# Batched experts on one core: two experts' weight matrices in one transfer, layers in pairs of experts

## The chip, the core and the metric

The kernel runs on one core of a Trainium2 chip. The time is that of one execution on the device, in microseconds (us); the lower the better. Several executions give a median. Beside them one execution was recorded by the hardware profiler, and every row below is from that one.

Five engines work side by side and meet at semaphores: TensorE (PE, matmuls; its weight loads are PEld), VectorE (DVE), ScalarE (ACT), GpSimd (POOL) and SyncE (SP). POOL and SP also issue DMA transfers, which 16 DMA engines carry out. An issuing engine takes its instructions in order: a transfer that must wait for a buffer holds up all that stands behind it in the same engine's list.

## What is computed

Eight experts, each a two-layer network with a ReLU between, on 256 rows each:

```
x  : 8 x 256 x 512     w1 : 8 x 512 x 2048     w2 : 8 x 2048 x 512     (all f32)
h   = relu(x[e] @ w1[e])
out[e] = h @ w2[e]                                                     (f32)
```

One weight matrix of one expert is 4.19 MB in f32. There are sixteen of them, 67.1 MB; x is another 4.19 MB and the output 4.19 MB. On the chip the weights, x and h are held in bf16, so a matrix takes 2.1 MB (the profile's "2048 KB"), 16 KB of each of 128 partitions. A transfer issued by POOL converts f32 to bf16 on the way; one issued by SP doesn't.

## The kernel before

**Loads.** `load_w1(e)` (line 69) brings w1 of one expert with one transfer, `load_w2(e)` (line 75) w2 of one expert; w2 of experts 6 and 7 comes in two pieces each. All go out on POOL's queue and are served one after the other. w1 and w2 have a pool of three buffers each (`WB = 3`), so six matrices of 2.1 MB can be on the chip or on their way. The fourth w1 can only be issued when the first layer of expert 0 has read its buffer, and so on.

**x.** x comes in groups (`GROUPS`): expert 0 alone, expert 1 alone, 2 and 3, 4 to 7. Experts 0 and 1 come through SP in f32 with one transfer each (line 145) and are cast to bf16 on ACT (lines 155 and 156); the others come through POOL (line 65). `transpose_x(g)` turns a group with PE transposes and copies the result out of PSUM on DVE and ACT.

**Layers.** `first_layer(e)` makes 64 matmuls of 256 columns (line 110) into four PSUM tiles, each of which ACT or DVE writes out with the ReLU as part of `ht[e]`, bf16. `second_layer(e)` makes 32 matmuls of 512 columns (line 130) into two PSUM tiles, which DVE and ACT copy (lines 137 and 138) into `o_sb`, f32. `ht` has three buffers.

**Stores.** The last 16 partitions of expert 0 leave through SP (line 169). Experts 1 to 4 (line 141) and the other 112 partitions of expert 0 (line 190) leave through POOL's queue, issued after the last weights. Experts 5 to 7 leave in one transfer through SP at the very end (line 193).

**Order.** The order is written out by hand, and each engine takes its own instructions in the order of the text. On PE, leaving out transposes: first 0, second 0, first 1, second 1, first 2, second 2, first 3, second 3, first 4, second 4, first 5, first 6, first 7, second 5, second 6, second 7. On POOL's queue: w1 0, w2 0, x of 2 and 3, w1 1, w2 1, x of 4 to 7, w1 2, w2 2, w1 3, w2 3, w1 4, w2 4, w1 5, w1 6, w1 7, w2 5, w2 6 (two pieces), w2 7 (two pieces), then the two stores.

Of the kernel before, what the change touches and what calls it, by code (L numbers as in the profile page):

```python
# [9 lines left out]
@with_exitstack  # L10
def kernel(
    ctx: ExitStack,
    tc: tile.TileContext,
    x: bass.AP,
    w1: bass.AP,
    w2: bass.AP,
    out: bass.AP,
):
    nc = tc.nc
    P = 128  # L20
    bf = mybir.dt.bfloat16
    f32 = mybir.dt.float32
    relu = mybir.ActivationFunctionType.Relu

    E, C, H = x.shape
    F = w1.shape[2]
    MT = C // P
    KT1 = H // P
    KT2 = F // P
    FB = 4  # L30
    WB = 3


    GROUPS = ((0, 1), (1, 1), (2, 2), (4, 4))


    w1_r = w1.rearrange("e (p kt) n -> e p kt n", p=P)
    w2_r = w2.rearrange("e (p kt) n -> e p kt n", p=P)
    out_r = out.rearrange("e (p mt) n -> p e mt n", p=P)

    const = ctx.enter_context(tc.tile_pool(name="const", bufs=1))
    wpool = ctx.enter_context(tc.tile_pool(name="weights", bufs=WB))
    hpool = ctx.enter_context(tc.tile_pool(name="hidden", bufs=3))
    ps_h = ctx.enter_context(tc.tile_pool(name="ps_h", bufs=2, space=bass.MemoryType.PSUM))
    ps_o = ctx.enter_context(tc.tile_pool(name="ps_o", bufs=4, space=bass.MemoryType.PSUM))


    ctx.enter_context(tc.manual_schedule())

    w1_sb, w2_sb, ht = {}, {}, {}  # L50
    group_of = {e: g for g, (e0, n) in enumerate(GROUPS) for e in range(e0, e0 + n)}
    x_f = const.tile([P, 2, MT, H], f32, name="x_f")
    x_b = [const.tile([P, n * MT, H], bf, name=f"x_b{g}") for g, (_, n) in enumerate(GROUPS)]
    xt = [const.tile([P, KT1, MT, n * P], bf, name=f"xt{g}") for g, (_, n) in enumerate(GROUPS)]
    o_sb = const.tile([P, E, MT, H], f32, name="out_sb")
    identity = const.tile([P, P], bf, name="identity")

    def x_rows(g):
        e0, n = GROUPS[g]
        return x[e0:e0 + n].rearrange("e c k -> (e c) k").rearrange(  # L60
            "(p j) k -> p j k", p=P
        )

    def load_x(g):
        nc.gpsimd.dma_start(x_b[g][:], x_rows(g))  # L65

    def load_w1(e):
        w1_sb[e] = wpool.tile([P, KT1, F], bf, tag="w1", name="w1_sb")
        nc.gpsimd.dma_start(w1_sb[e][:], w1_r[e])  # L69

    def load_w2(e):
        w2_sb[e] = wpool.tile([P, KT2, H], bf, tag="w2", name="w2_sb")
        cuts = {E - 2: (0, 8, 16), E - 1: (0, 9, 16)}.get(e, (0, KT2))
        for lo, hi in zip(cuts, cuts[1:]):
            nc.gpsimd.dma_start(w2_sb[e][:, lo:hi, :], w2_r[e, :, lo:hi, :])  # L75

    def transpose_x(g, blocks=None):


        n = GROUPS[g][1]  # L80
        J = n * MT
        KB = 8 // J
        for b in blocks if blocks is not None else range(KT1 // KB):
            pt = ps_o.tile([P, KB, J, P], bf, tag="ps_o", name="pt_tr")
            for i in range(KB):
                for j in range(J):
                    nc.tensor.transpose(  # L87
                        pt[:, i, j, :], x_b[g][:, j, b * KB + i::KT1], identity[:]
                    )
            for i in range(KB) if n > 1 else (slice(0, KB),):  # L90
                if n > 1:
                    src = pt[:, i].rearrange("p (l m) q -> p l m q", m=MT)
                    dst = xt[g][:, b * KB + i].rearrange("p m (q l) -> p l m q", l=n)
                    flip = b * KB + i
                else:
                    src, dst, flip = pt[:, i], xt[g][:], g
                if flip % 2:
                    nc.scalar.copy(dst, src)  # L98
                else:
                    nc.vector.tensor_copy(dst, src)  # L100

    def first_layer(e, between=()):
        g = group_of[e]
        i0 = (e - GROUPS[g][0]) * P
        ht[e] = hpool.tile([P, KT2, C], bf, tag="ht", name="ht_sb")
        for q in range(KT2 // FB):
            ph = ps_h.tile([P, FB, C], f32, tag="ps_h", name="pt_h")
            for i in range(FB):
                for kt in range(KT1):
                    nc.tensor.matmul(  # L110
                        ph[:, i, :],
                        w1_sb[e][:, kt, FB * q + i::KT2],
                        xt[g][:, kt, :, i0:i0 + P],
                        start=(kt == 0),
                        stop=(kt == KT1 - 1),
                    )
            if q % 2:
                nc.vector.tensor_relu(ht[e][:, FB * q:FB * (q + 1), :], ph[:])  # L118
            else:
                nc.scalar.activation(ht[e][:, FB * q:FB * (q + 1), :], ph[:], relu)  # L120
            if between:
                between.pop(0)()

    def second_layer(e):
        po = [
            ps_o.tile([P, H], f32, tag="ps_o", name=f"pt_o{mt}") for mt in range(MT)
        ]
        for kt in range(KT2):
            for mt in range(MT):
                nc.tensor.matmul(  # L130
                    po[mt][:],
                    ht[e][:, kt, mt * P:(mt + 1) * P],
                    w2_sb[e][:, kt, :],
                    start=(kt == 0),
                    stop=(kt == KT2 - 1),
                )
        nc.vector.tensor_copy(o_sb[:, e, 0, :], po[0][:])  # L137
        nc.scalar.copy(o_sb[:, e, 1, :], po[1][:])  # L138

    def store(e0, e1):  # L140
        nc.gpsimd.dma_start(out_r[:, e0:e1], o_sb[:, e0:e1])  # L141


    for e in (0, 1):
        nc.sync.dma_start(x_f[:, e], x_rows(e))
    load_w1(0)
    make_identity(nc, identity)
    load_w2(0)
    load_x(2)
    load_w1(1)  # L150
    load_w2(1)
    load_x(3)
    load_w1(2)
    load_w2(2)
    nc.scalar.copy(x_b[0][:], x_f[:, 0])  # L155
    nc.scalar.copy(x_b[1][:], x_f[:, 1])  # L156
    transpose_x(0)

    first_layer(0)
    load_w1(3)  # L160
    transpose_x(1)
    second_layer(0)
    load_w2(3)
    first_layer(1)
    load_w1(4)
    transpose_x(2)
    second_layer(1)
    for p in range(112, P, 4):
        nc.sync.dma_start(out_r[p:p + 4, 0], o_sb[p:p + 4, 0])
    load_w2(4)  # L170
    first_layer(2, [lambda kt=kt: transpose_x(3, [kt]) for kt in range(KT1)])
    load_w1(5)
    second_layer(2)
    first_layer(3)
    load_w1(6)
    second_layer(3)
    first_layer(4)
    load_w1(7)
    load_w2(5)
    load_w2(6)  # L180
    second_layer(4)
    load_w2(7)


    for e in (5, 6, 7):
        first_layer(e)


    store(1, 5)
    nc.gpsimd.dma_start(out_r[:112, 0], o_sb[:112, 0])  # L190
    for e in (5, 6, 7):
        second_layer(e)
    nc.sync.dma_start(out_r[:, 5:8], o_sb[:, 5:8])


# [28 lines left out]
```

## Time and profile before

| | |
|---|---|
| median of the runs | 183.04 us |
| the three runs | 183.12, 181.7, 183.04 us |
| span of the profiled execution | 180.0 us |
| PE busy | 127.5 us (71%) in 825 instructions |
| PEld busy | 90.1 us (50%) |
| DVE / ACT busy | 31.8 / 31.6 us (18% each) |
| POOL busy | 12.7 us (7%) |
| chain that ended last, by engine | DMA 45%, PE 40%, unknown queue 8% |

The span runs from the first recorded instruction to the last event of the execution; the time of a run also holds what lies before and after it. PE's busy time is a modelled one, and its idle time matters only where the end of the program waits for it. The rows of the profile that bear on the change are shown in the prediction. In a timeline row stand the start, the duration, engine and line, operation, tile written <- tiles read, the count, and in brackets the idle time before it with what ended it. In a row of windows stand the stretch, its length, each engine's busy time with its instruction count, the granted TensorE clock (1.00 is full), the mean busy share of the DMA engines and the GB/s that they moved, counted on the side of the chip's own memory (bf16 for weights).

### The profile page before, as it was taken

How to read it: one execution, taken by the hardware profiler on the slowest of the kernel's cores; microseconds unless marked ns; L12 is line 12 of the kernel's file. 1: busy time of each engine (PE TensorE's matmuls, PEld its weight loads, DVE VectorE, ACT ScalarE, POOL GpSimd, SP SyncE). 2: the span in 40 equal slices, each digit the busy share in tenths (PEclk: the TensorE clock that was granted, in tenths of full speed). 3: DMA queues.
4: the chain of work that ended last, by engine and by line, in shares of the span. 5: the costliest groups of instructions: out<-in, count | busy, mean ns of one | idle time of the engine just before them, and what ended most of it. 6: DMA issues, size and time to landing. Idle time of an engine off the chain costs nothing.

```text
span 180.0 us, 1823 instructions
## 1 busy us (share of the span) xinstructions
PE 127.5 (71%) x825; PEld 90.1 (50%) x832; DVE 31.8 (18%) x29; ACT 31.6 (18%) x32; POOL 12.7 (7%) x28
## 2 busy tenths in 40 slices
PE   0206999059993199987869497949895876997930
PEld 0105964048840189637723395428795873442410
DVE  0100220101411018610401022010423050101010
ACT  3300240102231026612200022012222220101010
POOL 7300010100101000100100004021010000000000
PEclk9999999957999659999999789996999999999995
DMA  5998998999999999999999999999999999999996
GB/s 210 256 226 182 233 229 178 233 211 215 200 244 204 222 218 208 218 215 229 204 222 218 218 211 211 229 208 222 215 222 208 215 215 204 224 213 209 334 411 248
DMA packets 4262, 40.47 MB, mean 225 GB/s; under 512 B 416, under 2 KB 416, under 8 KB 1952
## 3 DMA queue, kind: packets, MB, share of 16 engines
q0 software_dynamic: 3536, 37.68, 95.7%
q1 hardware_dynamic: 720, 2.69, 3.9%
q8 instruction: 6, 0.10, 0.2%
HBM read 71.30 MB, written 4.19 MB: 419 GB/s over the span
## 4 chain that ended last, share of the span: by engine, by line
DMA 45%; PE 40%; another core or an unknown queue 8%; POOL 1%; issue 1%; ACT 0%; POOLq 0%
DMA w_sb<-in_w_dram 45%; PE pt_o L130 19%; PE pt_h L110 19%; PE pt_tr L87 2%; POOL w_sb L69 0%; ACT out_sb L138 0%; POOL x_b L65 0%; POOL w_sb L75 0%; POOL identity masks.py:199 0%; POOL identity masks.py:197 0%; POOLq masks.py:199 0%; POOLq L208 0%
## 5 line engine op out<-in xcount | busy, mean ns | idle before, releaser
L110 PE MATMUL pt_h<-xt,w_sb 128*128 128x256 bf16 x512 | 67.6, 299 | 31.9 <-DMA w_sb<-in_w_dram 31.9
L110 PEld LDWEIGHTS <-w_sb 128*128 128x128 bf16 x512 | 60.9, 148 | 39.1 <-DMA w_sb<-in_w_dram 35.0
L130 PE MATMUL pt_o<-w_sb,ht_sb 128*128 128x512 bf16 x249 | 56.2, 379 | 7.9 <-DMA w_sb<-in_w_dram 7.4
L130 PEld LDWEIGHTS <-ht_sb 128*128 128x128 bf16 x256 | 24.9, 98 | 37.4 <-issue 7.2
L118 DVE TENSOR_SCALAR ht_sb<-pt_h 128x1024 bf16<-128x1024 f32 x16 | 19.7, 1229 | 69.3 <-PE pt_h L110 69.3
L120 ACT ACTIVATE ht_sb<-pt_h 128x1024 bf16<-128x1024 f32 x16 | 16.5, 1031 | 72.6 <-PE pt_h L110 72.6
L138 ACT COPY out_sb<-pt_o 128x512 f32<-128x512 f32 x8 | 4.7, 586 | 58.9 <-PE pt_o L130 58.9
L137 DVE COPY out_sb<-pt_o 128x512 f32<-128x512 f32 x8 | 5.5, 692 | 53.6 <-PE pt_o L130 53.6
L69 POOL DMA_DIRECT2D w_sb<-in_w_dram x8 | 4.4, 556 | 87.4 <-PE pt_h L110 86.6
L100 DVE COPY xt<-pt_tr 128x1024 bf16<-128x1024 bf16 (+1 forms) x5 | 7.1, 1449 | 18.2 <-PE pt_tr L87 18.2
L87 PE MATMUL pt_tr<-identity,x_b 128*128 128x128 bf16 x64 | 5.6, 242 | 5.3 <-ACT x_b L155 5.3
L98 ACT COPY xt<-pt_tr 128x1024 bf16<-128x1024 bf16 (+1 forms) x5 | 7.4, 1494 | 6.9 <-PE pt_tr L87 4.3
L87 PEld LDWEIGHTS <-x_b 128*128 128x128 bf16 x64 | 4.9, 121 | 5.4 <-ACT x_b L155 5.3
L75 POOL DMA_DIRECT2D w_sb<-in_w_dram x10 | 5.4, 547 | 20.3 <-PE pt_o L130 20.3
L155 ACT CAST x_b<-x_f 128x1024 bf16<-128x1024 f32 x1 | 1.0, 1045 | 2.1 <-DMA x_f<-in_x_dram 2.1
L155 ACT ACT_TABLE_LOAD x1 | 1.3, 1283 | 0.7 <-PEq L208 0.7
L190 POOL DMA_DIRECT2D out_dram<-out_sb x1 | 0.5, 545 | 8.6 <-DMA w_sb<-in_w_dram 8.6
L65 POOL DMA_DIRECT2D x_b<-in_x_dram x2 | 1.1, 550 | 0.0
L156 ACT CAST x_b<-x_f 128x1024 bf16<-128x1024 f32 x1 | 1.0, 1047 | 0.1
L141 POOL DMA_DIRECT2D out_dram<-out_sb x1 | 0.8, 768 | 1.8 <-DMA w_sb<-in_w_dram 1.8
masks.py:199 POOL TENSOR_SCALAR_AFFINE_SELECT identity<-identity 128x128 bf16<-128x128 bf16 x1 | 0.3, 288 | 0.1
masks.py:197 POOL MEMSET identity<- 128x128 bf16 x1 | 0.2, 225 | 0.0
(4 smaller groups left out, 0.4 us busy)
## 6 DMA issues: line engine op xcount, KB each, us to landing
w_sb<-in_w_dram POOLq DMA_DIRECT2D x14, 2048.0 KB, 45.4
w_sb<-in_w_dram POOLq DMA_DIRECT2D x2, 1024.0 KB, 45.4
out_dram<-out_sb POOLq DMA_DIRECT2D x1, 2048.0 KB, 53.0
out_dram<-out_sb SPq DMA_DIRECT2D x1, 1536.0 KB, 6.0
w_sb<-in_w_dram POOLq DMA_DIRECT2D x1, 1152.0 KB, 46.6
x_f<-in_x_dram SPq DMA_DIRECT2D x2, 512.0 KB, 3.7
x_b<-in_x_dram POOLq DMA_DIRECT2D x1, 1024.0 KB, 47.9
w_sb<-in_w_dram POOLq DMA_DIRECT2D x1, 896.0 KB, 50.3
```

Of the source, the lines that this page charges most:

```text
L69: nc.gpsimd.dma_start(w1_sb[e][:], w1_r[e])
L75: nc.gpsimd.dma_start(w2_sb[e][:, lo:hi, :], w2_r[e, :, lo:hi, :])
L87: nc.tensor.transpose(pt[:, i, j, :], x_b[g][:, j, b * KB + i::KT1], identity[:])
L98: nc.scalar.copy(dst, src)
L100: nc.vector.tensor_copy(dst, src)
L110: nc.tensor.matmul(ph[:, i, :], w1_sb[e][:, kt, FB * q + i::KT2], xt[g][:, kt, :, i0:i0 + P], start=(kt == 0), stop=(kt == KT1 - 1),)
L118: nc.vector.tensor_relu(ht[e][:, FB * q:FB * (q + 1), :], ph[:])
L120: nc.scalar.activation(ht[e][:, FB * q:FB * (q + 1), :], ph[:], relu)
L130: nc.tensor.matmul(po[mt][:], ht[e][:, kt, mt * P:(mt + 1) * P], w2_sb[e][:, kt, :], start=(kt == 0), stop=(kt == KT2 - 1),)
L137: nc.vector.tensor_copy(o_sb[:, e, 0, :], po[0][:])
L138: nc.scalar.copy(o_sb[:, e, 1, :], po[1][:])
L155: nc.scalar.copy(x_b[0][:], x_f[:, 0])
```

## The change

The three buffers for w1 and the three for w2 become three buffers of double size with one common tag; each holds the same matrix of two neighbouring experts. `load_w1(e)` and `load_w2(e)` bring both experts with one transfer; only w2 of 6 and 7 still comes as three pieces (6 whole, 7 in two) into one double buffer. The groups of x are 0 and 1, 2 and 3, 4 to 7; x of experts 0 and 1 comes with one transfer on SP and is cast with one instruction. `ht` has four buffers in place of three. On PE the layers run in pairs: first 0, first 1, second 0, second 1, first 2, first 3, second 2, second 3, first 4, first 5, first 6, first 7, second 4, second 5, second 6, second 7. On POOL's queue: w1 of 0 and 1, w2 of 0 and 1, x of 2 and 3, w1 of 2 and 3, w2 of 2 and 3, x of 4 to 7, w1 of 4 and 5, w1 of 6 and 7, w2 of 4 and 5, w2 of 6, w2 of 7 (two pieces), then the two stores as before. The three double buffers are taken in turn, so the fourth transfer (w2 of 2 and 3) waits for the first layer of expert 1, the fifth for the second layer of expert 1, the sixth for the first layer of expert 3, the seventh for the second layer of expert 3, and w2 of 6 and 7 for the first layer of expert 5.

```diff
-    GROUPS = ((0, 1), (1, 1), (2, 2), (4, 4))
+    PAIR = 2
+    GROUPS = ((0, 2), (2, 2), (4, 4))
...
-    hpool = ctx.enter_context(tc.tile_pool(name="hidden", bufs=3))
+    hpool = ctx.enter_context(tc.tile_pool(name="hidden", bufs=4))
...
-    x_f = const.tile([P, 2, MT, H], f32, name="x_f")
+    x_f = const.tile([P, 2 * MT, H], f32, name="x_f")
...
-    def load_w1(e):
-        w1_sb[e] = wpool.tile([P, KT1, F], bf, tag="w1", name="w1_sb")
-        nc.gpsimd.dma_start(w1_sb[e][:], w1_r[e])
+    def pair_tile():
+        return wpool.tile([P, PAIR, KT1 * F], bf, tag="w", name="w_sb")
+
+    def load_w1(e):
+        w = pair_tile()
+        nc.gpsimd.dma_start(
+            w[:], w1_r[e:e + PAIR].rearrange("e p kt n -> p e (kt n)")
+        )
+        for i in range(PAIR):
+            w1_sb[e + i] = w[:, i].rearrange("p (kt n) -> p kt n", n=F)
...
-    def load_w2(e):
-        w2_sb[e] = wpool.tile([P, KT2, H], bf, tag="w2", name="w2_sb")
-        cuts = {E - 2: (0, 8, 16), E - 1: (0, 9, 16)}.get(e, (0, KT2))
-        for lo, hi in zip(cuts, cuts[1:]):
-            nc.gpsimd.dma_start(w2_sb[e][:, lo:hi, :], w2_r[e, :, lo:hi, :])
+    def load_w2(e, cuts=None):
+        w = pair_tile()
+        for i in range(PAIR):
+            w2_sb[e + i] = w[:, i].rearrange("p (kt n) -> p kt n", n=H)
+        if cuts is None:
+            nc.gpsimd.dma_start(
+                w[:], w2_r[e:e + PAIR].rearrange("e p kt n -> p e (kt n)")
+            )
+            return
+        for i, lo, hi in cuts:
+            nc.gpsimd.dma_start(w2_sb[e + i][:, lo:hi, :], w2_r[e + i, :, lo:hi, :])
...
+    nc.sync.dma_start(x_f[:], x_rows(0))
+    load_w1(0)
+    make_identity(nc, identity)
+    load_w2(0)
+    load_x(1)
+    load_w1(2)
+    nc.scalar.copy(x_b[0][:], x_f[:])
+    transpose_x(0)
+    first_layer(0)
+    first_layer(1)
+    load_w2(2)
+    load_x(2)
+    second_layer(0)
+    second_layer(1)
+    load_w1(4)
+    for p in range(112, P, 4):
+        nc.sync.dma_start(out_r[p:p + 4, 0], o_sb[p:p + 4, 0])
+    transpose_x(1)
+    first_layer(2)
+    first_layer(3)
+    load_w1(6)
+    second_layer(2)
+    second_layer(3)
+    load_w2(4)
+    transpose_x(2)
+    first_layer(4)
+    first_layer(5)
+    load_w2(6, ((0, 0, 16), (1, 0, 9), (1, 9, 16)))
+    first_layer(6)
+    first_layer(7)
+    second_layer(4)
+    second_layer(5)
+    store(1, 5)
+    nc.gpsimd.dma_start(out_r[:112, 0], o_sb[:112, 0])
+    second_layer(6)
+    second_layer(7)
+    nc.sync.dma_start(out_r[:, 5:8], o_sb[:, 5:8])
```

The second-layer and first-layer functions are the same in both kernels; `transpose_x` loses the branch for groups of one expert.

More of the change, by code (lines that the diff above doesn't have):

```diff
@@ L141, in store @@
         nc.gpsimd.dma_start(out_r[:, e0:e1], o_sb[:, e0:e1])
-    for e in (0, 1):
-        nc.sync.dma_start(x_f[:, e], x_rows(e))
+    nc.sync.dma_start(x_f[:], x_rows(0))
     load_w1(0)
@@ L148 @@
     load_w2(0)
[L149 to L152, printed above, removed]
+    load_x(1)
     load_w1(2)
-    load_w2(2)
-    nc.scalar.copy(x_b[0][:], x_f[:, 0])
-    nc.scalar.copy(x_b[1][:], x_f[:, 1])
+    nc.scalar.copy(x_b[0][:], x_f[:])
     transpose_x(0)
     first_layer(0)
-    load_w1(3)
-    transpose_x(1)
+    first_layer(1)
+    load_w2(2)
+    load_x(2)
     second_layer(0)
-    load_w2(3)
-    first_layer(1)
+    second_layer(1)
     load_w1(4)
-    transpose_x(2)
-    second_layer(1)
     for p in range(112, P, 4):
         nc.sync.dma_start(out_r[p:p + 4, 0], o_sb[p:p + 4, 0])
[L170 to L173, printed above, removed]
+    transpose_x(1)
+    first_layer(2)
     first_layer(3)
     load_w1(6)
+    second_layer(2)
     second_layer(3)
+    load_w2(4)
+    transpose_x(2)
     first_layer(4)
-    load_w1(7)
-    load_w2(5)
-    load_w2(6)
+    first_layer(5)
+    load_w2(6, ((0, 0, 16), (1, 0, 9), (1, 9, 16)))
+    first_layer(6)
+    first_layer(7)
     second_layer(4)
-    load_w2(7)
-    for e in (5, 6, 7):
-        first_layer(e)
+    second_layer(5)
     store(1, 5)
     nc.gpsimd.dma_start(out_r[:112, 0], o_sb[:112, 0])
-    for e in (5, 6, 7):
-        second_layer(e)
+    second_layer(6)
+    second_layer(7)
     nc.sync.dma_start(out_r[:, 5:8], o_sb[:, 5:8])
```

12 lines of the change are left out of this document (4 added, 8 removed).

## The prediction

> **What bounds the kernel now.** I read the busy shares by slice first, then TensorE's timeline, then POOL's, then the last microseconds.
>
> ```profile
> DMA  5998998999999999999999999999999999999996
> GB/s 210 256 226 182 233 229 178 233 211 215 200 244 204 222 218 208 218 215 229 204 222 218 218 211 211 229 208 222 215 222 208 215 215 204 224 213 209 334 411 248
> q0 software_dynamic: 3536, 37.68, 95.7%
> HBM read 71.30 MB, written 4.19 MB: 419 GB/s over the span
> ```
>
> The DMA engines are full in nearly every slice, and 95.7% of their time is POOL's queue, the weights. The 210 to 220 GB/s are counted in bf16; on the HBM side it is twice that. So the kernel is bound by the stream of weights, and TensorE waits for it:
>
> ```profile
> 15.08 9.16 PE L110 MATMUL pt_h<-xt,w_sb 128*128 128x256 bf16 x64 [8.78 <-DMA w_sb<-in_w_dram]
> ...
> 37.95 9.65 PE L110 MATMUL pt_h<-xt,w_sb 128*128 128x256 bf16 x64 [6.08 <-DMA w_sb<-in_w_dram]
> ...
> 62.36 3.63 PE L110 MATMUL pt_h<-xt,w_sb 128*128 128x256 bf16 x16 [6.96 <-DMA w_sb<-in_w_dram]
> ...
> 81.95 7.22 PE L110 MATMUL pt_h<-xt,w_sb 128*128 128x256 bf16 x64 [1.48 <-DMA w_sb<-in_w_dram]
> 91.65 7.07 PE L130 MATMUL pt_o<-w_sb,ht_sb 128*128 128x512 bf16 x31 [2.48 <-DMA w_sb<-in_w_dram]
> 101.32 8.71 PE L110 MATMUL pt_h<-xt,w_sb 128*128 128x256 bf16 x64 [2.60 <-DMA w_sb<-in_w_dram]
> 111.00 7.07 PE L130 MATMUL pt_o<-w_sb,ht_sb 128*128 128x512 bf16 x31 [0.97 <-DMA w_sb<-in_w_dram]
> 120.68 8.87 PE L110 MATMUL pt_h<-xt,w_sb 128*128 128x256 bf16 x64 [2.61 <-DMA w_sb<-in_w_dram]
> 130.40 7.21 PE L110 MATMUL pt_h<-xt,w_sb 128*128 128x256 bf16 x64 [0.85 <-DMA w_sb<-in_w_dram]
> 140.11 7.21 PE L110 MATMUL pt_h<-xt,w_sb 128*128 128x256 bf16 x64 [2.50 <-DMA w_sb<-in_w_dram]
> 149.79 13.97 PE L130 MATMUL pt_o<-w_sb,ht_sb 128*128 128x512 bf16 x62 [2.47 <-DMA w_sb<-in_w_dram]
> 165.00 4.06 PE L130 MATMUL pt_o<-w_sb,ht_sb 128*128 128x512 bf16 x18 [1.24 <-DMA w_sb<-in_w_dram]
> 169.26 3.18 PE L130 MATMUL pt_o<-w_sb,ht_sb 128*128 128x512 bf16 x14 [0.20 <-DMA w_sb<-in_w_dram]
> ```
>
> Each row's start is the landing of a matrix, so these rows are the clock of the stream. From 111.00 (w2 of 4) to 149.79 (w2 of 5) four matrices land, one per 9.70 us: 4.19 MB in 9.7 us is 432 GB/s, without a gap. A first layer takes 7.2 us at full clock and a second layer 7.0 (13.97 for two; a few matmul records are missing), so TensorE needs 14.2 us per expert while the stream needs 19.4: TensorE is ahead. What counts is how much of TensorE's work is left when the stream ends. Before, all is done behind the last piece (169.26) but 14 matmuls, 3.18 us.
>
> **The stream after the change.** The same bytes go through the same queue. Is it ever dry? A transfer is issued when its buffer comes free:
>
> ```profile
> 2.45 0.55 POOL L75 DMA_DIRECT2D w_sb<-in_w_dram  x1
> ...
> 24.53 0.54 POOL L69 DMA_DIRECT2D w_sb<-in_w_dram  x1 [18.35 <-PE pt_h L110]
> ...
> 121.27 0.77 POOL L141 DMA_DIRECT2D out_dram<-out_sb  x1 [1.85 <-DMA w_sb<-in_w_dram]
> w_sb<-in_w_dram POOLq DMA_DIRECT2D x14, 2048.0 KB, 45.4
> ```
>
> A weight transfer lands 45.4 us (median) after its issue, so nearly five matrices are always queued. I date the pairs by counting bytes. In units of one matrix (9.7 us; x of experts 4 to 7 is half a unit, 4.85): w1 of 0 and 1 is one unit behind 15.08, so 24.8; w2 of 0 and 1 44.1. At 62.36 five matrices and all of x had landed; w1 of 2 and 3 is six without x of 4 to 7, so 62.36 + 9.7 - 4.85 = 67.2. w2 of 2 and 3 is eight, without that x: 91.65 - 4.85 = 86.8. w1 of 4 and 5 is ten matrices and all x, as 111.00 was; w1 of 6 and 7 is twelve, as 130.40 was; w2 of 4 and 5 is fourteen, the same set of bytes but for order as at 149.79; w2 of 7 ends at 169.26 again.
>
> Now the buffers. First layers 0 and 1 end at 24.8 + 9.2 + 7.2 = 41.2 and let w2 of 2 and 3 out; what is queued lasts to 67.2. Second layers 0 and 1 end at 44.1 + 14.0 = 58.1 (w1 of 4 and 5 is needed at 91.6, when x of 4 to 7 is through); first layers 2 and 3 at 67.2 + 9.65 + 7.2 = 84.1 (needed 111.0); second layers 2 and 3 at 100.8 (needed 130.4); first layers 4 and 5 at 111.0 + 9.65 + 7.2 = 127.9 (needed 149.8). The smallest reserve is 21.9 us, the last one. So the start of TensorE at 24.8 in place of 15.08 costs nothing: the queue covers it. If that cover were gone, the missing microseconds would be added one to one.
>
> **Edits of no or little price.** x of 0 and 1 as one transfer and one cast:
>
> ```profile
> 4.16 1.04 ACT L155 CAST x_b<-x_f 128x1024 bf16<-128x1024 f32 x1 [2.13 <-DMA x_f<-in_x_dram]
> ```
>
> This was over at 5.2 and is now needed at 24.8, so a later landing and a longer cast cost nothing. Fewer issues: POOL is not on the path. A pair has 256 runs of 16 KB where one matrix had 128; the store of line 141, with 512 shorter ones, took 0.77 us to issue beside 0.55, so a pair costs at most 0.2 us more, once, at the start. Sum: 0 to 0.2, I take 0. The stores of line 141 and 190 now wait on POOL for second layer 4 (about 159 in place of 121.27), with no load behind them and before 169.26, so they keep their place in the queue. On SP the small stores of line 169 wait for second layer 0 of the new order (about 51); only the last store stands behind them. That the stream loses or wins up to 1.1 us at its beginning (15.08 + two and a quarter units is 36.9, the row says 37.95) stays as an uncertainty of 1.1 either way.
>
> Fewer transfers in the stream: behind 149.79 two matrices came as four pieces and took 19.47 us to 169.26, beside 19.40 for two whole ones; an extra piece costs 0.04 us. Seven fewer transfers before w2 of 4 and 5 (14 become 7): 0.3 us won. [...]
>
> **The tail, where the price is.** At 149.8 before, TensorE had three second layers to do (5, 6, 7), paced by the stream. After the change second layer 4 stands behind first layer 7 too, and w2 of 4 comes only with w2 of 5: four remain, and nothing of them can start earlier. Four at 13.97 per two are 27.9 us. w2 of 6 (159.5) and of 7 (169.26) have landed by the time they are wanted (163.8 and 170.8 at the earliest), so TensorE is now the bound of the end.
>
> And it starts cold. Stretches of the first layers of 1 and 4 and of the three last second layers:
>
> ```profile
> 37.95:48.30 10.35, 10.35 (x80) 9.18 (x81) 1.88 (x2) 2.05 (x2) 0.40 (x1) 0.75 0.99 212
> 101.32:111.00 9.68, 8.71 (x64) 7.88 (x65) 2.15 (x2) 2.05 (x2) 0.67 (x2) 0.84 1.02 217
> 149.79:165.00 15.21, 13.87 (x63) 6.17 (x64) 1.38 (x2) 1.17 (x2) 0.00 (x0) 1.00 1.02 214
> ```
>
> Behind an idle gap of 6.08 us the granted clock was 0.75 over the stretch and the 64 matmuls took 9.65 in place of 7.21 (2.44 lost); behind 2.60, 8.71 (1.5 lost); behind 2.47 and 2.50 nothing. In the tail, first layer 6 starts at 130.4 after a gap of 2.5 (7.2 to 8.9 us), first layer 7 ends at 144.8 to 146.5, and the gap to 149.8 is 3.3 to 5.0 us: between the rows that lost 1.5 and 2.44. I take 2.0, bounds 0 and 2.5.
>
> The end of TensorE: 149.8 + 27.9 + 2.0 = 179.7. Behind it:
>
> ```profile
> 172.48 0.59 ACT L138 COPY out_sb<-pt_o 128x512 f32<-128x512 f32 x1 [8.09 <-PE pt_o L130]
> 173.09 0.41 SPq L193 DMA_DIRECT2D out_dram<-out_sb  x1
> out_dram<-out_sb SPq DMA_DIRECT2D x1, 1536.0 KB, 6.0
> 175.00:176.00 1.00, 0.00 (x0) 0.00 (x0) 0.00 (x0) 0.00 (x0) 0.00 (x0) 1.00 1.00 406
> 178.00:179.00 1.00, 0.00 (x0) 0.00 (x0) 0.00 (x0) 0.00 (x0) 0.00 (x0) 0.50 0.23 94
> ```
>
> The last copy 0.6, the store's landing 6.0, then 0.9 to the span's end of 180.0. Before, the POOL stores (2048 KB and 448 KB) waited in the queue behind w2 of 7 and shared the engines with the last store. After, they run 169.3 to about 175.5 while TensorE still works, and the last store is alone: 1.57 MB at 406 GB/s are 3.9 us, plus about 0.8 each at start and end (0.9 before, from the last busy stretch to landing): 5.5, bounds 4.7 and 6.0. Sum: 179.7 + 0.6 + 5.5 + 0.9 = 186.7; less 0.3 for fewer transfers, 186.4. That is 6.4 us above this profile's 180.0.
>
> The profiled span is 3.04 us under the median of 183.04 (runs 181.7 to 183.12); I carry that difference over: 189.4 us.
>
> **Rivals.**
>
> A fixed cost per transfer in the stream (other side, faster). Two x transfers of 512 KB on SP took 3.7 us to land,
>
> ```profile
> x_f<-in_x_dram SPq DMA_DIRECT2D x2, 512.0 KB, 3.7
> ```
>
> while their 1.05 MB need 2.4 at the stream's rate, so 1.3 us are not bytes. If each weight transfer paid that in the stream, seven fewer would land w2 of 4 and 5 at 140.7, and the whole tail with it: 189.7 (my sum without the 0.3) - 9.1 = 180.6, faster by 1.3%. It decides from about 1.0 us per transfer (6.7 us over seven). Against it stand the 0.04 us per extra piece and the 432 GB/s without a gap. Chance 4%.
>
> Slower reading of pairs. One transfer now alternates, partition by partition, between two matrices 4.19 MB apart in HBM, a pattern that no row shows. The slowest stretch of the stream is 15.08 to 37.95, 22.87 us for 2.25 units (21.8), 5% under its rate. At that rate all through to w2 of 4 and 5 (134.7 us from 15.08), the tail starts 6.7 us later: about 196. The nearest rows (every other matrix at 9.7) speak against it. Chance 8%. [...]
>
> Starvation by coarse buffers. Three double buffers come free in steps of two matrices; with a reserve of 21.9 us TensorE would have to be later than I date it by all of that, and only beyond this point is each microsecond added. Five further, say: 194. Chance 2%.
>
> The forecast, the tail of four second layers: 86%.
>
> **From here to the numbers.** Inside the forecast the parts reach from 186.6 (no cold start, the store at 4.7) to 190.4 (2.5 and 6.0); with 1.1 us for the start of the stream either way and about 1 us by which three runs wander (181.7 to 183.12), which seldom all fall on one side, 186.5 to 192.5. The slow-reading case at 2% in place of 5% lies inside, at 192. I leave out its far part, starvation and the fixed cost. A measurement of this kernel tells about 1% from no change. Faster by over 1%: the fixed cost, 4%. Within 1%: that cost at half its size together with a warm start, 3%. Slower: 93%.
>
> **What would show it.** First matmuls of layer 0 at about 25; w1 of 6 and 7 and w2 of 4 and 5 landing within 1.5 us of 130 and 150; no slice of the DMA row under 9 before 169; the issue of w2 of 6 at about 128, some 20 us ahead of need; second layers 4 to 7 without a wait for a transfer between, about 30 us together, their first microseconds at half the granted clock; the last store alone. Wrong would be: a landing of w2 of 4 and 5 at 143 or earlier (fixed cost), at 153 or later with a full DMA row (slow reading), or a hole in that row (starvation).

## The result and the profile after

The changed kernel takes 187.84 us in the median (186.42 to 188.74, 6 runs), the kernel before 181.69 us (181.54 to 183.12, 6 runs). The ratio is 1.0324, with a 95% interval of 1.0297 to 1.0352: slower by 3.2%. Ratios, here and below, leave out runs over 1.5% above the fastest of the same kernel; medians and ranges hold all runs. The profiled execution has a span of 186.2 us (180.0 before) and took 188.03 us, so 1.83 us lie outside the span.

TensorE's timeline of the changed kernel, in the form in which that of before was shown:

```profile
7.74 1.89 PE L101 MATMUL pt_tr<-identity,x_b 128*128 128x128 bf16 x16 [7.74 <-ACT x_b L160]
25.56 16.85 PE L120 MATMUL pt_h<-xt,w_sb 128*128 128x256 bf16 x128 [15.93 <-DMA w_sb<-in_w_dram]
45.72 16.84 PE L140 MATMUL pt_o<-w_sb,ht_sb 128*128 128x512 bf16 x64 [3.32 <-DMA w_sb<-in_w_dram]
62.40 1.06 PE L101 MATMUL pt_tr<-identity,x_b 128*128 128x128 bf16 x16
67.54 15.86 PE L120 MATMUL pt_h<-xt,w_sb 128*128 128x256 bf16 x128 [4.08 <-DMA w_sb<-in_w_dram]
87.50 16.43 PE L140 MATMUL pt_o<-w_sb,ht_sb 128*128 128x512 bf16 x64 [4.11 <-DMA w_sb<-in_w_dram]
103.78 1.95 PE L101 MATMUL pt_tr<-identity,x_b 128*128 128x128 bf16 x32
111.13 16.73 PE L120 MATMUL pt_h<-xt,w_sb 128*128 128x256 bf16 x128 [5.40 <-DMA w_sb<-in_w_dram]
130.49 15.61 PE L120 MATMUL pt_h<-xt,w_sb 128*128 128x256 bf16 x128 [2.63 <-DMA w_sb<-in_w_dram]
149.91 29.47 PE L140 MATMUL pt_o<-w_sb,ht_sb 128*128 128x512 bf16 x128 [3.81 <-DMA w_sb<-in_w_dram]
```

Each row is now a pair, and each pair waits for its transfer. The stream itself is as fast as before: when w1 of all experts and w2 of 0 to 5 had landed, it was 149.79 before and is 149.91 now. Only what is left to do at that moment differs: four second layers in one piece (29.47 us), with no wait for a transfer inside. The DMA rows show the same from the other side:

```profile
DMA  5999999999999999999999999999999999999417
GB/s 209 231 194 218 222 222 225 218 208 204 218 225 223 223 215 208 211 218 211 236 225 204 211 208 225 222 225 215 211 208 215 225 222 214 200 206 377 203 55 282
```

Behind the first slice none is under 9 until the stream ends. Then comes what the kernel before didn't have, a hole (4 and 1 tenths, slices of 4.65 us): the DMA engines have nothing left but the last store, and that waits for TensorE. The end in windows and in issues:

```profile
151.00:152.00 1.00, 1.00 (x4) 0.42 (x3) 0.00 (x0) 0.00 (x0) 0.00 (x0) 0.50 0.84 180
155.00:156.00 1.00, 1.00 (x6) 0.48 (x5) 0.00 (x0) 0.00 (x0) 0.00 (x0) 1.00 1.13 246
174.00:175.00 1.00, 1.00 (x6) 0.49 (x5) 0.00 (x0) 0.00 (x0) 0.00 (x0) 1.00 0.52 213
176.00:177.00 1.00, 1.00 (x6) 0.47 (x5) 0.00 (x0) 0.00 (x0) 0.00 (x0) 1.00 0.00 0
181.00:182.00 1.00, 0.00 (x0) 0.00 (x0) 0.00 (x0) 0.00 (x0) 0.00 (x0) 1.00 1.00 406
```

```profile
179.42 0.58 ACT L148 COPY out_sb<-pt_o 128x512 f32<-128x512 f32 x1 [6.32 <-PE pt_o L140]
180.03 0.41 SPq L193 DMA_DIRECT2D out_dram<-out_sb  x1
out_dram<-out_sb SPq DMA_DIRECT2D x1, 1536.0 KB, 5.3
```

About half a microsecond behind 149.91 the granted clock falls to 0.50 (4 matmuls of a second layer per us in place of 6); from about 154 on it is 1.00. The DMA engines are done at about 174.5 (busy for half of the stretch from 174 to 175) and idle until the last store goes out at 180.03, 6.94 us later than before (173.09); alone on the engines it lands in 5.3 us in place of 6.0. 6.94 - 0.7 is the 6.2 us by which the span grew.

### The profile page after: what moved, and what is told of

It reads as the page before. It is cut to its first block, busy times and chain, and to the rows that moved or that the text cites. A ratio compares the mean times of both kernels' runs of the same rounds, so it can differ in the third digit from the quotient of the medians.

```text
span 186.2 us, 1816 instructions
## 1 busy us (share of the span) xinstructions
PE 132.4 (71%) x832; PEld 91.5 (49%) x832; DVE 32.6 (18%) x30; ACT 31.7 (17%) x32; POOL 9.8 (5%) x20
## 4 chain that ended last, share of the span: by engine, by line
DMA 62%; PE 34%; issue 1%; ACT 0%; POOLq 0%
DMA w_sb<-in_w_dram 62%; PE pt_o L140 25%; PE pt_h L120 9%; ACT out_sb L148 0%; POOLq L208 0%; POOLq masks.py:199 0%
## 5 line engine op out<-in xcount | busy, mean ns | idle before, releaser
L120 PE MATMUL pt_h<-xt,w_sb 128*128 128x256 bf16 x512 | 65.0, 296 | 28.0 <-DMA w_sb<-in_w_dram 28.0
L140 PE MATMUL pt_o<-w_sb,ht_sb 128*128 128x512 bf16 x256 | 62.7, 412 | 11.2 <-DMA w_sb<-in_w_dram 11.2
L140 PEld LDWEIGHTS <-ht_sb 128*128 128x128 bf16 x256 | 26.6, 104 | 46.7 <-issue 21.1
L101 PE MATMUL pt_tr<-identity,x_b 128*128 128x128 bf16 x64 | 4.9, 242 | 7.7 <-ACT x_b L160 7.7
L110 DVE COPY xt<-pt_tr 128x512 bf16<-128x512 bf16 (+1 forms) x6 | 7.5, 1308 | 8.9 <-PE pt_tr L101 8.8
L108 ACT COPY xt<-pt_tr 128x512 bf16<-128x512 bf16 (+1 forms) x6 | 7.5, 1310 | 2.9 <-DVE xt L110 2.5
L84 POOL DMA_DIRECT2D w_sb<-in_w_dram x3 | 2.2, 718 | 57.9 <-PE pt_h L120 38.1
L73 POOL DMA_DIRECT2D w_sb<-in_w_dram x4 | 3.0, 749 | 39.8 <-PE pt_h L120 20.1
L89 POOL DMA_DIRECT2D w_sb<-in_w_dram x3 | 1.6, 551 | 23.2 <-PE pt_h L120 23.2
L160 ACT CAST x_b<-x_f 128x2048 bf16<-128x2048 f32 x1 | 1.9, 1897 | 3.8 <-DMA x_f<-in_x_dram 3.8
## 6 DMA issues: line engine op xcount, KB each, us to landing
w_sb<-in_w_dram POOLq DMA_DIRECT2D x7, 4096.0 KB, 45.6
```

The source lines that it names most:

```text
L73: nc.gpsimd.dma_start(w[:], w1_r[e:e + PAIR].rearrange("e p kt n -> p e (kt n)"))
L84: nc.gpsimd.dma_start(w[:], w2_r[e:e + PAIR].rearrange("e p kt n -> p e (kt n)"))
L101: nc.tensor.transpose(pt[:, i, j, :], x_b[g][:, j, b * KB + i::KT1], identity[:])
L120: nc.tensor.matmul(ph[:, i, :], w1_sb[e][:, kt, FB * q + i::KT2], xt[g][:, kt, :, i0:i0 + P], start=(kt == 0), stop=(kt == KT1 - 1),)
L140: nc.tensor.matmul(po[mt][:], ht[e][:, kt, mt * P:(mt + 1) * P], w2_sb[e][:, kt, :], start=(kt == 0), stop=(kt == KT2 - 1),)
L160: nc.scalar.copy(x_b[0][:], x_f[:])
```

## The experiments

All ratios are to the kernel before, run beside it on the same chip; the changed kernel stands at 1.0324. "The start" below is that of second layer 4. In the expectations "tail theory" is the forecast, four second layers left behind a late landing; "fixed cost", "slow reading of pairs" and "starvation" are the rivals of the prediction.

**w2 of experts 4 and 5 in two transfers.**

```diff
-    load_w2(4)
+    load_w2(4, ((0, 0, 16), (1, 0, 16)))
```

> The changed kernel with w2 of experts 4 and 5 as two transfers (one per expert) into the same double buffer; all else as changed. Tail theory: w2 of 4 lands one matrix earlier, near 140, so second layer 4 starts when first layer 7 ends (about 146.1), without a gap and without a cold clock, and four second layers take 28.1 us: TensorE ends near 174.3, span near 181.3, 4.9 us under the changed kernel, ratio to the kernel before about 1.007. Fixed cost per transfer: one more transfer makes it 1 us slower. Slow reading of pairs: one pair fewer of seven, 1 us at most.

Measured: 182.28 us in the median, ratio 1.0023 (1.0006 to 1.0039). TensorE's timeline:

```profile
131.08 15.87 PE L120 MATMUL pt_h<-xt,w_sb 128*128 128x256 bf16 x128 [3.77 <-DMA w_sb<-in_w_dram]
146.79 27.79 PE L140 MATMUL pt_o<-w_sb,ht_sb 128*128 128x512 bf16 x125
```

The second row has no wait in brackets: second layer 4 follows first layer 7 at once. It starts 3.1 us earlier and runs at full clock (of the 40 slices of its profile, each from there to the end of TensorE has a granted clock of 9 tenths, 90% or more). The profiled span, 181.4, is the 181.3 expected; the nine other executions were shorter still (180.0 to 181.2), so the ratio is below the expected 1.007. In the profiled one, first layers 6 and 7 took 15.87 us with the clock at 6 tenths in the slice from 131.5 to 136.1, where they took 14.2 in other traces (14.19 at a mean clock of 1.00 in the next experiment). Whether that is the difference no trace shows. This one split takes away 3.0 of the 3.2%.

**Matmuls that only keep the clock up.** 28 matmuls between first layer 7 and second layer 4; nobody reads their result.

```diff
     first_layer(7)
+    fill = ps_o.tile([P, H], f32, tag="ps_o", name="pt_fill")
+    for _ in range(28):
+        nc.tensor.matmul(
+            fill[:, :C], w1_sb[7][:, 0, 0:P], xt[2][:, 0, :, 3 * P:4 * P],
+            start=True, stop=True,
+        )
     second_layer(4)
```

> The changed kernel with 28 more matmuls of 256 columns on TensorE between first layer 7 and second layer 4, into a PSUM tile that nobody reads (3.2 us of the 3.8 us gap). Cold-clock part of the tail theory: second layer 4 starts at the same time (149.9) but at full granted clock; the four second layers take 28.1 in place of 29.5 us, span 1.4 to 1.9 us shorter (about 184.5), ratio to before about 1.024. If the clock is not the cause of the 29.5: no change, 1.032.

Measured: 186.08 us, ratio 1.0232 (1.0215 to 1.0249), span 184.4.

```profile
144.51 3.22 PE L187 MATMUL pt_fill<-xt,w_sb 128*128 128x256 bf16 x28
149.81 27.79 PE L140 MATMUL pt_o<-w_sb,ht_sb 128*128 128x512 bf16 x125 [2.08 <-DMA w_sb<-in_w_dram]
```

The start is the same, the four layers take 27.8 in place of 29.5, at a mean granted clock of 1.00 in place of 0.94. So 1.7 us, 0.9 of the 3.2%, are the cold clock: work added to TensorE made the kernel faster.

**Every pair as two transfers**, order and buffers as changed.

```diff
-        nc.gpsimd.dma_start(
-            w[:], w1_r[e:e + PAIR].rearrange("e p kt n -> p e (kt n)")
-        )
         for i in range(PAIR):
+            nc.gpsimd.dma_start(
+                w[:, i], w1_r[e + i].rearrange("p kt n -> p (kt n)")
+            )
```

(and w2 in the same way)

> The changed kernel, its order of layers and its double buffers, but every weight pair as two transfers of one matrix each. Tail theory: first layers start earlier, w2 of 4 is there near 140, and the end is again the last piece at 169.3 plus 14 matmuls: span near 180, ratio to before 1.000 within 0.005. Fixed cost per transfer: seven more transfers before w2 of 5, 7 to 9 us slower than the changed kernel. Slow reading of pairs: the landing of w2 of 5 moves earlier than the 149.9 of the changed kernel.

Measured: 181.99 us, ratio 1.0028 (1.0000 to 1.0057).

```profile
149.84 7.07 PE L141 MATMUL pt_o<-w_sb,ht_sb 128*128 128x512 bf16 x31 [1.10 <-DMA w_sb<-in_w_dram]
159.53 15.67 PE L141 MATMUL pt_o<-w_sb,ht_sb 128*128 128x512 bf16 x63 [2.63 <-DMA w_sb<-in_w_dram]
```

The loss is gone, with the same layers and buffers. The first row is the landing of w2 of 5: 149.84, beside 149.91 with seven pairs. Seven transfers more cost nothing and seven pairs fewer won nothing: a fixed cost in the stream and a slower reading of pairs both fall. The profiled execution was the longest (span 182.0; eight of the ten have 180.1 to 180.5). In it the clock fell to 0.50 behind the gap of 2.63 us (160.5 to 163.5), and second layers 6 and 7 took 15.67 us in place of 13.97.

**Each w1 pair in four transfers.**

```diff
-        nc.gpsimd.dma_start(
-            w[:], w1_r[e:e + PAIR].rearrange("e p kt n -> p e (kt n)")
-        )
+        for kt in range(KT1):
+            nc.gpsimd.dma_start(
+                w[:, :, kt * F:(kt + 1) * F],
+                w1_r[e:e + PAIR, :, kt, :].rearrange("e p n -> p e n"),
+            )
```

> The changed kernel with each w1 pair as four transfers, each a quarter of both matrices (2 runs of 8 KB in HBM per partition and transfer); the first layers read all four quarters from their first matmuls on, so nothing can start earlier. Tail theory, with 0.04 us per extra piece: twelve more transfers cost 0.5 us at most, ratio to before 1.032 to 1.036. Fixed cost of about 1.3 us per transfer in the stream: 15 us slower, ratio about 1.11. If runs of 8 KB in place of 32 KB are read slower, w2 of 4 and 5 lands later than 149.9 by that.

Measured: 188.52 us, ratio 1.0342 (1.0298 to 1.0386).

```profile
150.52 0.49 PE L142 MATMUL pt_o<-w_sb,ht_sb 128*128 128x512 bf16 x1 [2.71 <-DMA w_sb<-in_w_dram]
```

In five traces of the changed kernel, or of variants that leave its transfers alone, w2 of 4 and 5 lands at 149.42 to 149.91. Here it is 0.6 to 1.1 us later with twelve transfers more: at most 0.09 us each, where a fixed cost of 1.3 us would have made 15. Part of it can be the spread between executions: w1 of 6 and 7 landed at 131.12 here, and at 131.08 in the first experiment, which up to there has no transfer more than the changed kernel.

**The order alone, in the kernel before.** Single transfers as they were; `ht` gets four buffers, and second layer 4 moves behind first layer 7.

```diff
-    hpool = ctx.enter_context(tc.tile_pool(name="hidden", bufs=3))
+    hpool = ctx.enter_context(tc.tile_pool(name="hidden", bufs=4))
...
     load_w2(6)
+    for e in (5, 6, 7):
+        first_layer(e)
     second_layer(4)
     load_w2(7)
...
-    for e in (5, 6, 7):
-        first_layer(e)
```

> The kernel before with its single transfers, and of the change only this: second layer 4 is moved behind first layer 7 (four hidden buffers as in the change; w2 of 7 is then issued after second layer 4). Tail theory: four second layers remain at 147.4, without a gap: TensorE ends near 175.5 in place of 172.5, last store alone, span near 182.3, ratio 1.012 (1.008 to 1.017). So the order alone would be about two fifths of the loss, and the late landing of w2 of 4 with its gap and cold clock the rest. If the pair transfers were the whole cause: ratio 1.000.

Measured: 184.34 us, ratio 1.0127 (1.0065 to 1.0189), span 182.1.

```profile
140.40 7.21 PE L110 MATMUL pt_h<-xt,w_sb 128*128 128x256 bf16 x64 [2.48 <-DMA w_sb<-in_w_dram]
147.45 27.79 PE L130 MATMUL pt_o<-w_sb,ht_sb 128*128 128x512 bf16 x125
```

With the weights of expert 4 long there, the order alone loses 1.3%: four second layers from 147.45. In this kernel's order of transfers w1 of 7 lands only at 140.40 (w2 of 4 is ahead of w1 of 5 to 7), and first layer 7 cannot end sooner. In the kernels with four second layers in one piece, the last store leaves 28.4 us behind the start at full clock (147.45 to 175.89 here, 146.79 to 175.22 in the first experiment, 149.81 to 178.25 with the added matmuls; the clock has 9 tenths in every slice there) and 30.1 in the changed kernel (149.91 to 180.03). The cold clock can cost more than there: 31.2 in the first run with less reserve below (149.42 to 180.59; 5 tenths in the slice from 149.4 to 154.1) and 31.3 in the second with x in two transfers (150.25 to 181.57; 5 and 8 tenths in the slices from 150.2 to 159.6).

**Less reserve.** The first attempt did not do what it was meant to: a double buffer was allocated ahead of w2 of 6 and 7 and left unused, so that these would take the next one.

```diff
+    pair_tile()
     load_w2(6, ((0, 0, 16), (1, 0, 9), (1, 9, 16)))
```

> The changed kernel with one of the three double buffers skipped in the rotation, so that w2 of 6 and 7 goes into the buffer of w1 of 6 and 7 and waits for the first layer of expert 7 (about 146) in place of expert 5 (128.2): the reserve before the stream runs dry falls from 22 us to about 4. Tail theory: w2 of 6 still lands near 160, four us before second layer 6 wants it (164.6); no change of the time, ratio to before 1.029 to 1.035. Starvation: if the changed kernel is slower because coarse buffers come free late, taking 18 us more of the reserve makes it much slower, by 5 us or more.

The issue stood at 126.79, no later than in the changed kernel (128.16): the unused buffer was given out again. It is a repeat of that kernel: 188.01 us, ratio 1.0338 (1.0278 to 1.0398). The second attempt puts a real wait on POOL, a copy of one column of `ht[7]`:

```diff
-    load_w2(6, ((0, 0, 16), (1, 0, 9), (1, 9, 16)))
     first_layer(6)
     first_layer(7)
+    probe = const.tile([P, 1], bf, name="probe")
+    nc.gpsimd.tensor_copy(probe[:], ht[7][:, KT2 - 1, 0:1])
+    load_w2(6, ((0, 0, 16), (1, 0, 9), (1, 9, 16)))
```

> The changed kernel with a copy of one column of the hidden tile of expert 7 on POOL, and the issue of w2 of 6 and 7 behind it: the issue moves from about 128 to about 148, so the reserve before the stream runs dry falls from 22 us to about 2. Tail theory: w2 of 6 lands by 161, three us before second layer 6 wants it, and w2 of 7 likewise; the time stays that of the changed kernel, ratio to before 1.029 to 1.039, with at most a small hole in the DMA row near 150. Starvation theory (coarse buffers that come free late are what slows the changed kernel): 5 us slower or more, ratio above 1.055.

Measured: 187.56 us, ratio 1.0326 (1.0310 to 1.0343).

```profile
146.08 1.64 POOL L89 DMA_DIRECT2D w_sb<-in_w_dram  x3 [0.31 <-issue]
```

```profile
147.00:149.00 2.00, 0.00 (x0) 0.00 (x0) 0.00 (x0) 0.00 (x0) 0.72 (x2) 1.00 0.80 156
```

The issue moved by 18 us, to 3.3 us ahead of the landing of w2 of 4 and 5 (149.42 here); the DMA share from 147 to 149 is 0.80, a dip but no hole. The time is the changed kernel's. The reserve had 18 us to spare; starvation falls as a cause.

**The two last pairs split.** w1 of 6 and 7 and w2 of 4 and 5 come as two transfers each, five pairs stay. (`load_w1` with `True` issues one transfer for each of the two experts; its body is left out here.)

```diff
-    load_w1(6)
+    load_w1(6, True)
...
-    load_w2(4)
+    load_w2(4, ((0, 0, 16), (1, 0, 16)))
```

> The changed kernel with only two pairs split: w1 of 6 and 7 and w2 of 4 and 5 as two transfers each; the five pairs before them stay. Tail theory: first layer 6 starts at once behind first layer 5 (127.5), first layer 7 ends near 142, second layers 4 to 7 are paced by the stream again: the time of the kernel before, ratio 1.000 within 0.005 (up to 1.010 where a gap of 2.6 us cools the clock before second layer 6). Fixed cost or slow reading of pairs: five pairs are still there, so a part of the 3.2% would remain or the sign turn.

Measured: 183.36 us, ratio 1.0061 (1.0027 to 1.0095). The runs lie in two groups, 181.8 to 182.0 (3) and 183.1 to 183.5 (7). The profile is of the upper one:

```profile
110.64 30.16 PE L126 MATMUL pt_h<-xt,w_sb 128*128 128x256 bf16 x256 [6.28 <-DMA w_sb<-in_w_dram]
140.64 7.07 PE L146 MATMUL pt_o<-w_sb,ht_sb 128*128 128x512 bf16 x31
149.40 7.07 PE L146 MATMUL pt_o<-w_sb,ht_sb 128*128 128x512 bf16 x31 [1.69 <-DMA w_sb<-in_w_dram]
159.06 15.67 PE L146 MATMUL pt_o<-w_sb,ht_sb 128*128 128x512 bf16 x63 [2.60 <-DMA w_sb<-in_w_dram]
```

Four first layers run on end and the second layers are paced by the stream again, but TensorE is so far ahead of it that a gap of 2.60 us opens before second layer 6, and the last two layers take 15.67 us in place of 13.97 (the granted clock is 0.50 from 160 to 162).

**The same with 14 matmuls in that gap.**

```diff
+    fill = ps_o.tile([P, H], f32, tag="ps_o", name="pt_fill")
+    for _ in range(14):
+        nc.tensor.matmul(
+            fill[:, :C], w1_sb[7][:, 0, 0:P], xt[2][:, 0, :, 3 * P:4 * P],
+            start=True, stop=True,
+        )
     second_layer(6)
```

> The kernel with the two split pairs (w1 of 6 and 7, w2 of 4 and 5) and 14 more matmuls of 256 columns before second layer 6, into a PSUM tile that nobody reads, so that the gap of 2.6 us there falls to about 1.0. Cold-clock theory: its runs lay in two groups, 181.9 and 183.4, because that gap cools the clock in most executions; with the filler all lie near the lower one, 181.4 to 182.4, ratio to before 0.998 to 1.003. If the two groups have another cause they stay, ratio near 1.006.

Measured: 181.99 us (181.84 to 182.86, 12 runs), ratio 1.0014 (0.9990 to 1.0039).

```profile
156.85 1.69 PE L199 MATMUL pt_fill<-xt,w_sb 128*128 128x256 bf16 x14
159.63 13.99 PE L146 MATMUL pt_o<-w_sb,ht_sb 128*128 128x512 bf16 x64 [1.08 <-DMA w_sb<-in_w_dram]
```

The upper group is gone, though two of the twelve runs lie at 182.8 and 182.9, a little above what was expected. With five pairs kept the kernel is as fast as before, and no faster: in both, the last landings of the stream set the end.

**x of 0 and 1 in two transfers again.**

```diff
-    nc.sync.dma_start(x_f[:], x_rows(0))
+    for j in (0, 2):
+        nc.sync.dma_start(x_f[:, j:j + 2], x_rows(0)[:, j:j + 2])
...
-    nc.scalar.copy(x_b[0][:], x_f[:])
+    for j in (0, 2):
+        nc.scalar.copy(x_b[0][:, j:j + 2], x_f[:, j:j + 2])
```

> The changed kernel with x of experts 0 and 1 as two transfers and two casts again. All theories: it is needed at 25.5 and there at 8, no change, ratio to before 1.029 to 1.035; this checks the term that the prediction set to nothing.

Measured: 188.96 us, ratio 1.0389 (1.0329 to 1.0450), above the expected band, and 0.95 us above the repeat of the changed kernel on the same chip (188.01). Because that was not explained, the changed kernel and this one were run side by side:

> The changed kernel itself once more, as the partner of the next run. All theories: ratio to before 1.030 to 1.035.

> x of experts 0 and 1 as two transfers and two casts, in the changed kernel, on the same chip as the run before this one. If the one transfer of x is worth nothing, as predicted: the same ratio within 0.3%. If two transfers of shorter rows delay the start of the stream, as one profile hinted (w1 of 0 and 1 at 25.8 in place of 25.6): later landings all along by that, and up to 0.6% slower.

Measured: the changed kernel 187.54 us, ratio 1.0278 (1.0243 to 1.0313); x in two 188.39 us, ratio 1.0359 (1.0324 to 1.0393). The first profile with x in two transfers:

```profile
25.82 16.62 PE L120 MATMUL pt_h<-xt,w_sb 128*128 128x256 bf16 x128 [16.71 <-DMA w_sb<-in_w_dram]
...
150.28 0.55 PE L140 MATMUL pt_o<-w_sb,ht_sb 128*128 128x512 bf16 x1 [5.15 <-DMA w_sb<-in_w_dram]
```

w2 of 4 and 5 lands at 150.28 here and at 150.25 in the second profile, where the five traces named above had 149.42 to 149.91. Both comparisons of times point the same way, 0.95 and 0.85 us in the medians. That x in two transfers costs up to 0.9 us is still not shown. The runs of the second comparison overlap (185.83 to 188.90 beside 186.72 to 189.55), and the changed kernel's own ratio was 1.0324 the first time and 1.0278 here. The first experiment, with x in one transfer, had w1 of 6 and 7 as late (131.08) as the two profiles with x in two (130.93 and 130.78). The kernel before, with x in two, had w2 of 5 at 149.79. Why a stream starts early or late stays open: TensorE has turned x some 16 us before the weights come either way.

## Why the prediction was right

**The stream.** Predicted that the same bytes land at the same times: 24.8, 44.1, 67.2, 86.8, 111.0, 130.4, 149.8. Measured 25.56, 45.72, 67.54, 87.50, 111.13, 130.49, 149.91. The early ones came up to 1.6 us late, covered by the queue (a pair lands 45.6 us, in the median, behind its issue); the one that sets the end was off by 0.1. In the four repeats and variants that leave the transfers alone it came at 149.42 to 149.81, so it was met within 0.4. That a transfer has next to no price in the stream was right (at most 0.09 us each in the quarters, 0.04 predicted); the 0.3 us taken off for seven transfers fewer do not show (149.91 with pairs, 149.84 with single transfers).

**The reserve.** Predicted 21.9 us at the smallest; the issue of w2 of 6 and 7 at 128.2 stands 21.7 us before 149.91. Taking 18 us of it away changed nothing.

**The tail.** Four second layers from 149.8: predicted 27.9, measured 27.8 with the clock kept up. The gap ahead of them: 3.3 to 5.0 predicted, 3.81 measured. The cold clock: 2.0 taken, 1.7 measured. The last store alone: 5.5 taken, 5.3 measured. The sum was a span of 186.4, measured 186.2. That it fits to 0.2 us is in part luck of the execution: the cold clock, which the prediction bounded by 0 and 2.5, cost 2.7 and 2.9 us in two other traces (31.2 and 31.3 us from the start to the last store, in place of 28.4).

**What was mis-sized.** The difference between span and time. The prediction carried 183.04 - 180.0 = 3.04 us over; the profiled execution of the changed kernel shows 1.83 (188.03 - 186.2). The first three runs of the kernel before (two of them at 183) were high for it: over six runs the median is 181.69. By that term alone the 189.4 us came out 1.2 too high; the measured 187.84 lies in the range. The one transfer of x, set to nothing, may be worth up to 0.9 us, which is not shown; it would lie within the 1.1 us kept for the start of the stream.

**How the loss divides.** From 1.0324, full clock in the tail takes 0.9% away, and the landing of w2 of 4 by itself, which removes both the gap and the cold clock, 3.0%. What remains there (0.2%) is the price of the fourth second layer: w1 of 6 and 7 land near 131, first layer 7 ends before 147, and most of the added layer fits in before the stream ends. So in the changed kernel's order of transfers the later place of second layer 4 was nearly free, but for the landing of its weights together with those of expert 5. It is not free in every order: in the kernel before, where w1 of 7 lands at 140.40, the same move costs 1.3% (0.65 to 1.9%). The two traces start the four layers only 0.7 us apart (146.79 and 147.45), so a part of the difference between 0.2 and 1.3% stays open.

## What to carry to other kernels

Here the queue of transfers was full and the compute engine ahead of it, and pairing transfers neither saved nor cost time in the stream; it moved the moment at which the first half may be used to the landing of the second. That was free wherever the queue hid it (w2 of 5 landed at 149.91, beside 149.79 before), and nearly all of the loss came in the last stage. In such a kernel, keep the last transfers small and count what is left to compute when the last-but-one lands. To forecast such a change, count bytes up to each landing: the sum of bytes gave the decisive date within 0.4 us in five traces.

## What was not expected of the hardware

The clock is not decided by the length of a gap alone. Gaps of 2.60 and 2.63 us ahead of a layer cost 1.7 us (the runs with the two last pairs split and with single transfers; the clock was 0.50 from 160 to 162 and from 160.5 to 163.5), and in the first attempt at less reserve, a repeat of the changed kernel, one of 2.24 us cost as much (15.66 us for two second layers in place of 13.97; 7 and 8 tenths of the clock in the slices from 84.1 to 93.4):

```profile
86.35 15.66 PE L140 MATMUL pt_o<-w_sb,ht_sb 128*128 128x512 bf16 x62 [2.24 <-DMA w_sb<-in_w_dram]
```

In the other repeat two gaps of 2.79 and 3.77 us cost nothing, with the granted clock at 1.00 over both stretches behind them:

```profile
86.85 13.97 PE L140 MATMUL pt_o<-w_sb,ht_sb 128*128 128x512 bf16 x64 [3.77 <-DMA w_sb<-in_w_dram]
...
130.13 14.20 PE L120 MATMUL pt_h<-xt,w_sb 128*128 128x256 bf16 x128 [2.79 <-DMA w_sb<-in_w_dram]
```

Between 2.24 and 3.77 us it went either way. So the reading in the prediction that gaps of 2.47 and 2.50 us cost nothing holds for its own trace: in the first experiment the two second layers behind a gap of 2.50 (at 87.52) took 15.56 us in place of 13.97, with the clock at 6 tenths in the slice from 86.2 to 90.7, and in the order-alone run the one behind a gap of 2.47 (at 91.97) took 8.66 in place of 7.07, with 6 tenths from 91.1 to 95.6. What else decides is not shown. The clock may be why the changed kernel's runs spread over 2.3 us (186.42 to 188.74) and those with the added matmuls ahead of second layer 4 over 0.6 (185.85 to 186.44), but this is not shown: the four runs with the late issue, which keep the gap, lie within 0.35 (187.49 to 187.84).
